# The low parts of the Mamba layer's weights: subtracted by VectorE, or added by a transfer onto the negative high part

## The chip, the core and the metric

The kernel runs on one core of a Trainium2 chip. Five engines take part: TensorE multiplies matrices (in the profile PE for the products and PEld for the loads of the stationary operand), VectorE (DVE), ScalarE (ACT) and GpSimd (POOL) do the elementwise work, and SyncE (SP) begins most transfers; transfers themselves are moved by 16 DMA engines. Every engine works through its own instructions in the order in which the program gives them. The metric is the device time of one launch in microseconds (us); less is better.

## The reference, cut to what matters

A two-layer streaming encoder runs on 512 prompt frames and 32 sample frames, taken together as 544 columns. The first layer is a feed-forward half step, a Mamba-2 mixer, another feed-forward half step and a gated input embedding; the second layer has attention in the mixer's place. The change touches only the Mamba-2 mixer:

```python
def mamba2_mixer(h, ssm0, conv0, w_in, conv_w, conv_b, dt_bias, a_log, d_skip, norm_g, w_out):
    zxbcdt = h @ w_in
    z = zxbcdt[..., :D_INNER]
    ...
    xbc, conv_new = causal_dwconv(xbc, conv0, conv_w, conv_b)
    xbc = jax.nn.silu(xbc).astype(jnp.float32)
    ...
    y, s_fin = ssd_scan(xs * dt[..., None], dt * A, Bm, Cm, s0, chunk_len)
    y = y + xs * d_skip...
    y = y.reshape(b, L, D_INNER) * jax.nn.silu(z.astype(jnp.float32))
    ...
    out = y.astype(h.dtype) @ w_out
```

All of it is float32. The two products with `w_in` (1024 by 5152) and `w_out` (2048 by 1024) are what the change concerns: how their weights get into the form in which TensorE takes them.

## The kernel before

**High and low parts.** A float32 product is made from three products in the reduced type float32r: each weight tile `raw` (128 partitions by 1024 columns, 512 KB) is split into a high part `whi`, which is `raw` rounded to float32r, and a low part `wlo`, which is `raw` minus `whi`, rounded again. The activations are split likewise. `product` (line 282) then makes, for each 128 by 128 block, the products high by high, high by low and low by high, each in two halves of 272 columns: 48 matrix instructions for a tile.

**The Mamba stage.** `mamba` (line 938) lists its weight tiles in `units`, 58 of them: one for the time steps, 24 for the convolved inputs (for each of four groups B, C and four x tiles), 16 for the gates z, 16 for the output, and one that belongs to the feed-forward block that follows. `dense` (line 1115) goes through them in order and gives TensorE a tile's products as soon as the tile is split. The first tile comes split from the stage before, so 57 are split here. Beside the products runs the scan, `ssd` (line 1326), for four groups of five chunks each: transposes and small products on TensorE; on ScalarE the decays `ex` and `ab` by exponentials; on VectorE the evictions and multiplications by decays; on GpSimd the products `xw`, `ab` and `st`. For each chunk SyncE fetches `ab` (line 1163), a table of running sums, repeated to all partitions. The scan's results go through a gated norm (`gnorm`, line 1343) and become the activations of the output tiles.

**Feed.** The class `Feed` (line 311) has two chains. `fetch` (line 318) begins the transfer of tile after tile from SyncE into one of two `raw` buffers. `split` (line 330) waits for the tile, takes one of two `w` slots (a pair of buffers `whi` and `wlo`), copies `raw` into `whi` on ScalarE or GpSimd, subtracts on VectorE or GpSimd, and gives the `raw` buffer back. `dense` gives the `w` slot back when the tile's products are given out.

**What sets the order.** The order of each engine's instructions is made by a planner, the class `Plan` (line 65), while the program is built. Every piece of work is a chain, a generator that asks for slots, for events, or for time on an engine: `T`, `V`, `S`, `G` stand for TensorE, VectorE, ScalarE and GpSimd, `W` for VectorE without the port that it shares with GpSimd in the planner's account. `run` (line 137) always takes the step that can start first by the planner's own clock, among equals the chain of lowest rank, and writes down its instruction then. `copy` (line 306) and `either` (line 302) choose the engine that the planner holds to be less loaded, with GpSimd's time weighted by 7 in this stage. A transfer of a tile is booked as landing after 4.5 us, one of `ab` after 5.0 us. On the chip each engine keeps that order and waits where the planner's clock was wrong. The chain of `split` has rank -2, that of `fetch` -3, the scan's from 1 on, `dense` 50.

Of the kernel before, what the change touches and what calls it, by code (L numbers as in the profile page):

```python
# [5 lines left out]
F32R = mybir.dt.float32r  # L6
BF16 = mybir.dt.bfloat16
AF = mybir.ActivationFunctionType
ALU = mybir.AluOpType

P = 128
D = 1024
# [9 lines left out]
W = 547  # L22
# [22 lines left out]
NZB, NY, NYH = 1, 2, 4  # L45
# [19 lines left out]
class Plan:  # L65
# [9 lines left out]

    LAG = {"TT": 0.0, "TS": 0.2, "TV": 0.2, "TG": 0.23, "ST": 0.28, "SS": 0.143, "SV": 0.142, "SG": 0.17,
           "VT": 0.26, "VS": 0.128, "VV": 0.127, "VG": 0.155, "GT": 0.28, "GS": 0.075, "GV": 0.068, "GG": 0.096}
    LOAD = 1.3  # L80

    def __init__(self, slots, name):
        self.share = SHARE[name]
        self.busy = dict.fromkeys("TVSG", 0.0)
        self.port = 0.0
        self.slots = {k: [0.0] * n for k, n in slots.items()}
        self.events, self.chains, self.table = {}, [], None
# [27 lines left out]
    def start(self, c):  # L115
        kind, t = c["req"][0], c["t"]
        if kind == "get":
            free = self.slots[c["req"][1]]
            return max(t, min(free)) if free else None
        if kind == "wait":  # L120
            when = [self.events.get(e) for e in c["req"][1:]]
            return None if None in when else max([t] + when)
        kind, port = ("V", 0.0) if kind == "W" else (kind, self.port if kind in "VG" else 0.0)
        t = max(t + (self.LAG[c["on"] + kind] if c["on"] else 0.2), self.busy[kind], port)
        table = c["req"][3] if len(c["req"]) > 3 else None
        return t + (self.LOAD if table not in (None, self.table) else 0.0)

    def load(self, engine):

        kinds = "VW" if engine in "VW" else engine  # L130
        return self.busy["V" if engine == "W" else engine] + sum(c["req"][1] for c in self.chains if c["req"][0] in kinds)

    def pick(self, *options):
# [3 lines left out]
    def run(self):  # L137
        while self.chains:
            best = None
            for c in self.chains:  # L140
                t = self.start(c)
                if t is not None and (best is None or t < best[0] - 1e-9):
                    best = t, c
            assert best is not None, "no chain can go on"
            t, c = best
            kind = c["req"][0]
            if kind == "get":
                free = self.slots[c["req"][1]]
                free.remove(min(free))
                c["t"] = t  # L150
            elif kind == "wait":
                if t > c["t"]:
                    c["on"] = None
                c["t"] = t
            else:
                c["req"][2]()
                if len(c["req"]) > 3:
                    self.table = c["req"][3]
                if kind in "VG":
                    self.port = t + c["req"][1]  # L160
                kind = "V" if kind == "W" else kind
                c["t"] = self.busy[kind] = t + c["req"][1]
                c["on"] = kind
            self.step(c)
# [6 lines left out]
def s_cost(n, psum=False):  # L171
    return n / 1200.0 + (0.052 if psum else 0.094)


def v_cost(n):
    return n / 960.0 + 0.069


def _body(tc, io):
# [3 lines left out]
    class Engine:  # L183


        def __init__(self, name, engine):
            self.name, self.engine = name, engine
# [9 lines left out]
    V, S, G, TE = (Engine(n, e) for n, e in (("V", nc.vector), ("S", nc.scalar), ("G", nc.gpsimd), ("T", nc.tensor)))  # L197
# [4 lines left out]
    with ExitStack() as ctx:  # L202
# [66 lines left out]
        def weight_parts(pool=pool):  # L269
            return [pool.tile([P, 1024], F32R, tag=t, name=t, bufs=2) for t in ("whi", "wlo")]  # L270
# [27 lines left out]
        def split(dst_hi, dst_lo, src):  # L298
            S.activation(dst_hi, src, AF.Copy)
            V.tensor_tensor(out=dst_lo, in0=src, in1=dst_hi.bitcast(F32), op=ALU.subtract)  # L300

        def either(plan, cost_v, cost_g, emit):

            return plan.pick(("V", cost_v, lambda: emit(V)), ("G", cost_g, lambda: emit(G)))

        def copy(plan, n, out, src):

            return plan.pick(("S", s_cost(n), lambda: S.activation(out, src, AF.Copy)),
                             ("G", (0.055 + n / 960.0) * (1.0 if n <= 544 else 0.9), lambda: G.tensor_scalar(out, src, 1.0, 0.0, op0=ALU.mult, op1=ALU.add)))

        class Feed:


            def __init__(self, plan, aps, ready=(), here=0):
                self.plan, self.aps, self.ready, self.here = plan, aps, len(ready), len(ready) + here
                self.raw, self.loaded = {}, dict(enumerate(ready))

            def fetch(self):
# [11 lines left out]
            def split(self):  # L330
                for k in range(len(self.aps)):
                    if k < self.ready:
                        yield "get", "w"
                        yield "set", (self, k)
                        continue
                    yield "wait", (id(self), "raw", k)
                    yield "get", "w"
                    raw = self.raw[k]
                    hi = pool.tile([P, 1024], F32R, tag="whi", name="whi", bufs=2)
                    yield copy(self.plan, 1024, hi, raw)  # L340
                    lo = pool.tile([P, 1024], F32R, tag="wlo", name="wlo", bufs=2)
                    yield either(self.plan, v_cost(1024), 2.4, lambda e: e.tensor_tensor(out=lo, in0=raw, in1=hi.bitcast(F32), op=ALU.subtract))
                    self.loaded[k] = hi, lo
                    yield "put", "raw"
                    yield "set", (self, k)


        class Norm:
# [33 lines left out]
            def scale(self, psum, ring):  # L382
                if self.share is not None:
                    self.r = self.share.r
                else:
                    parts = ring() if ring else [self.acc]
                    if ring:
                        split(*parts, self.acc)
                    self.r = at_once(rsqrt_ops(psum(), parts, D, "r", sign=-1 if ring else 1))
                return self.r  # L390
# [505 lines left out]
        def sevens(i, norm, after, bank, tmp, ring, roles, **kw):  # L896
            slots = {f"b{k}": 1 for k in range(4)}
            slots.update({f"c{k}": 1 for k in range(4)})
            slots.update({"raw": 2, "w": Sevens.NW, "a11": 1, "a21": 1, "a22": 1, "a12": 1, "s3": 1, "s2": 1, "gu0": 1, "gu1": 1, "sq": 2, "acc": 1, "h": NH})
            return Sevens(Plan(slots, "ff"), i, norm, bank, tmp, ring, roles, after, **kw).run()  # L900
# [37 lines left out]
        def mamba(norm, after, ready, ahead):  # L938
            with tc.tile_pool(name="mt", bufs=1, reuse_waits="tile") as tmp, \
# [6 lines left out]
                def aux():  # L946
                    return pa.tile([P, 512], F32, tag="aux", name="aux")

                plan = Plan({"mm": 2, "aux": 4, "raw": 2, "w": 2, "cu": 2, "cv": 2, "grp": 2, "z": NZB, "y": NY, "yh": NYH,
                             "ab": 2, "ex": 2, "xd": 2, "xw": 2, "cb": 1, "btok": 1, "st": 3, "fade": 2}, "m")  # L950
                chunks = [(c * P, P) for c in range(NCH)] + [(TP, TS)]
                tok = tmp.tile([P, 5, 96], F32, tag="tok", name="tok")
# [147 lines left out]
                units = [(io["win"][40], "dt", 0, 0)]  # L1100
# [299 lines left out]
                        yield "wait", ("z", g, 0), *[("out", g, c) for c in range(5)]  # L1400
                        yield from gnorm(g)

                feed = Feed(plan, [u[0] for u in units], ready, 1)
                for g in range(NG):
                    plan.add(RSCAN * g + 1, ssd(g))
                    for c in range(5):
# [515 lines left out]
        def space(name, side=None):  # L1922
            st = ExitStack()
            return st, st.enter_context(tc.tile_pool(name=name, bufs=1, reuse_waits="tile", **({"side": side} if side else {})))

        def ring_of(pool, tag, n):
            return lambda: tuple(pool.tile([P, T], F32R, tag=tag + k, name=tag + k, bufs=n) for k in "hl")

        sp, psum, bank, roles = banks(START[0])
        st, tmp = space("ff")  # L1930
# [9 lines left out]
        ready = sevens(0, n00, nm0.ops, bank, tmp, ring_of(tmp, "h", NH), (2, 3, 1, 0), opened=opened, ahead=io["win"][40])  # L1940
        st.close()
        sp.close()
        n01 = Norm("f01")
        ready = mamba(nm0, n01.ops, ready, io["wgu"][1, 0, 0])

        kvp = ctx.enter_context(tc.tile_pool(name="kvp", bufs=1, reuse_waits="tile"))
# [18 lines left out]
        st, tmp = space("pl")  # L1965
# [12 lines left out]
        st, tmp = space("ff")  # L1978
        ready = sevens(2, n10, nm1.ops, bank, tmp, ring_of(tmp, "h", NH), roles(), first=first, ahead=io["wq"][0])
# [3 lines left out]
        ready = attention(nm1, n11.chunk, ready, io["wgu"][3, 0, 0], *kvs)  # L1983
# [3 lines left out]
        st, tmp = space("pl")  # L1987
# [124 lines left out]
```

## Time and profile before

| what | value |
|---|---|
| median of three runs | 2340.38 us (2337.31 to 2341.64) |
| the profiled execution's own time | 2335.02 us |
| its span, first to last instruction | 2332.9 us |
| busy in the span: PE, PEld | 2295.5 us, 2206.8 us |
| busy in the span: DVE, ACT, POOL | 1707.0 us, 1045.5 us, 599.3 us |
| read from HBM | 204.83 MB |
| transfers begun by GpSimd | none |

The times of the profile are those of one execution, in microseconds from its first instruction. An engine's busy time is the time in which it ran at least one of its instructions. Since matrix instructions overlap, PE shows as busy where it only drains; the loader PEld stands still as soon as the next product can't start, so its idle time tells more of TensorE's pauses. "Idle before" names the instruction whose end let the waiting one go.

### The profile page before, as it was taken

To read this page: it belongs to the slowest core of one execution; us is meant where nothing else is said; L and a number is where in the kernel's file an instruction comes from. 1 tells how busy PE (TensorE), PEld (TensorE's weight loads), DVE (VectorE), ACT (ScalarE), POOL (GpSimd) and SP (SyncE) were. 2 spreads that over 40 slices of the span, in tenths; PEclk is the share of its full clock that TensorE was granted. 3 is DMA by queue.
4 is the path that set the end of the run, shared out by engine and by line. 5 is a ranking of instruction groups with operands and counts; after the bars stand their busy time and mean duration, and the time that the engine had idled before them with its cause. 6 is when DMAs were issued, how large, how long until landed. Compare 5 with 4: busy or idle time off the path is not lost.

```text
span 2332.9 us, 42534 instructions
## 1 busy us (share of the span) xinstructions
PE 2295.5 (98%) x17750; PEld 2206.8 (95%) x17757; DVE 1707.0 (73%) x2237; ACT 1045.5 (45%) x1528; POOL 599.3 (26%) x570
## 2 busy tenths in 40 slices
PE   8999999999999999999999999999998999999997
PEld 8999999989899999999999999999964799999997
DVE  7677786689677676777857677777678686777857
ACT  5333334567555453333345433333478553333343
POOL 3322122144324122212211221211334122222214
PEclk9999999999999999999999999999999999999998
DMA  4233323333333232333233333232311132333232
GB/s 159 83 99 105 96 66 90 112 98 99 112 91 90 82 118 84 90 108 91 73 101 100 110 100 95 89 107 67 88 41 32 37 118 78 105 96 99 65 104 75
DMA packets 112176, 213.17 MB, mean 91 GB/s; under 512 B 12528, under 2 KB 34672, under 8 KB 111984
## 3 DMA queue, kind: packets, MB, share of 16 engines
q1 hardware_dynamic: 109104, 204.92, 29.5%
q10 hardware_dynamic: 2880, 5.53, 0.7%
q8 instruction: 140, 2.29, 0.4%
q14 instruction: 52, 0.43, 0.1%
HBM read 204.83 MB, written 5.60 MB: 90 GB/s over the span
## 4 chain that ended last, share of the span: by engine, by line
PE 89%; DVE 5%; ACT 2%; issue 2%; POOL 1%; DMA 1%; SPq 0%; DVEq 0%; ACTq 0%; POOLq 0%
PE mm L191 80%; PE z L191 5%; PE aux L191 2%; PE f L191 1%; DVE wlo L191 1%; PE o L191 1%; POOL ab L191 1%; DVE xl L191 1%; ACT whi L191 1%; DVE x L191 1%; DMA x<-in_x 0%; DVE sl L191 0%; DMA wraw<-in_wpg 0%; DVE fu L191 0%; POOL st L191 0%
## 5 line engine op out<-in xcount | busy, mean ns | idle before, releaser
L191 PE MATMUL mm<-xh,whi 128*128 128x272 f32 x2096 | 512.2, 292 | 0.8 <-ACT xh L191 0.4
L191 PE MATMUL mm<-xl,whi 128*128 128x272 f32 x2096 | 508.0, 290 | 4.4 <-DVE xl L191 4.4
L191 PE MATMUL mm<-xh,wlo 128*128 128x272 f32 x2096 | 505.9, 289 | 2.1 <-DVE wlo L191 2.1
L191 PEld LDWEIGHTS mm<-xh,whi 128*128 128x128 f32 x2096 | 358.1, 189 | 8.9 <-issue 7.0
L191 ACT ACTIVATE whi<-wraw 128x1024 fp32r<-128x1024 f32 (+3 forms) x219 | 188.0, 859 | 392.6 <-PE mm L191 271.7
L191 PEld LDWEIGHTS mm<-xl,whi 128*128 128x128 f32 x2096 | 358.2, 190 | 5.5 <-DVE xl L191 5.5
L191 PEld LDWEIGHTS mm<-xh,wlo 128*128 128x128 f32 x2096 | 358.0, 189 | 2.9 <-DVE wlo L191 2.9
L191 PE MATMUL mm<-xfh,whi 128*128 128x272 f32 x1152 | 332.0, 288 | 0.0
L191 PE MATMUL mm<-xfl,whi 128*128 128x272 f32 x1152 | 331.9, 288 | 0.0
L191 PE MATMUL mm<-xfh,wlo 128*128 128x272 f32 x1152 | 331.7, 288 | 0.0
L191 DVE TENSOR_TENSOR wlo<-wraw,whi 128x1024 fp32r<-128x1024 f32 (+3 forms) x253 | 258.5, 1022 | 71.0 <-ACT whi L191 53.4
L191 PE MATMUL mm<-hh,whi 128*128 128x272 f32 x1408 | 291.2, 288 | 0.0
L191 PE MATMUL mm<-hh,wlo 128*128 128x272 f32 x1408 | 291.0, 288 | 0.0
L191 PE MATMUL mm<-hl,whi 128*128 128x272 f32 x1408 | 290.7, 288 | 0.0
L191 ACT ACTIVATE whi<-a 128x1024 fp32r<-128x1024 f32 x126 | 133.8, 1062 | 310.9 <-PE mm L191 202.8
L191 DVE TENSOR_TENSOR wlo<-a,whi 128x1024 fp32r<-128x1024 f32 x144 | 176.5, 1226 | 102.1 <-ACT whi L191 68.8
L191 PEld LDWEIGHTS mm<-hl,whi 128*128 128x128 f32 x1408 | 221.2, 188 | 0.0
L191 PEld LDWEIGHTS mm<-hh,whi 128*128 128x128 f32 x1408 | 220.9, 188 | 0.0
L191 PEld LDWEIGHTS mm<-hh,wlo 128*128 128x128 f32 x1408 | 220.5, 188 | 0.2 <-DVE wlo L191 0.2
L191 PEld LDWEIGHTS mm<-xfh,wlo 128*128 128x128 f32 x1152 | 216.8, 188 | 0.0
L191 PEld LDWEIGHTS mm<-xfl,whi 128*128 128x128 f32 x1152 | 216.8, 188 | 0.0
L191 PEld LDWEIGHTS mm<-xfh,whi 128*128 128x128 f32 x1152 | 216.7, 188 | 0.0
(293 smaller groups left out, 4200.5 us busy)
## 6 DMA issues: line engine op xcount, KB each, us to landing
a<-in_wgu SPq DMA_DIRECT2D x144, 512.0 KB, 3.9
wraw<-in_wd SPq DMA_DIRECT2D x128, 256.0 KB, 2.7
wraw<-in_win SPq DMA_DIRECT2D x41, 512.0 KB, 3.6
wraw<-in_wgu SPq DMA_DIRECT2D x30, 512.0 KB, 3.6
wraw<-in_wd SPq DMA_DIRECT2D x32, 384.0 KB, 3.1
ab<-acs_d SPq DMA_DIRECT2D x16, 512.0 KB, 4.3
wraw<-in_wout SPq DMA_DIRECT2D x16, 512.0 KB, 3.6
wraw<-in_wpg SPq DMA_DIRECT2D x16, 512.0 KB, 3.6
```

The lines of the kernel that those rows point to most:

```text
L191: ins = getattr(self.engine, op)(*args, **kw)
```

## The change

In the Mamba stage alone, `Feed` gets a pool `third` and takes another way. ScalarE writes the negative high part into the low part's buffer (`lo`, an activation with scale -1 whose output type rounds). GpSimd then begins a transfer that reads the same weight tile from HBM a second time and adds it to that buffer. The high part is copied as before, on ScalarE or GpSimd. VectorE's subtraction (or GpSimd's) is gone. The planner books 0.9 us on GpSimd for beginning the transfer (the new kind `D`, which counts on GpSimd without the shared port) and counts the tile as ready 5.5 us later, by a chain of its own. The `raw` buffer goes back once both copies are made. There are three `w` slots instead of two, the third pair of buffers from the stage's own pool; the last three tiles use only the two old pairs, since these outlive the stage.

```diff
+    ON = {"W": "V", "D": "G"}
...
-        kind, port = ("V", 0.0) if kind == "W" else (kind, self.port if kind in "VG" else 0.0)
+        kind, port = (self.ON[kind], 0.0) if kind in "WD" else (kind, self.port if kind in "VG" else 0.0)
...
-        kinds = "VW" if engine in "VW" else engine
+        kinds = {"V": "VW", "W": "VW", "G": "GD", "D": "GD"}.get(engine, engine)
...
-                kind = "V" if kind == "W" else kind
+                kind = self.ON.get(kind, kind)
...
-            def __init__(self, plan, aps, ready=(), here=0):
-                self.plan, self.aps, self.ready, self.here = plan, aps, len(ready), len(ready) + here
+            def __init__(self, plan, aps, ready=(), here=0, third=None):
+                self.plan, self.aps, self.ready, self.here, self.third = plan, aps, len(ready), len(ready) + here, third
...
                     raw = self.raw[k]
+                    if self.third is not None:
+
+                        third = k % 3 == 2
+                        if third and k >= len(self.aps) - 3:
+                            yield "get", "w"
+                            third = False
+                        hi, lo = self.loaded[k] = (tuple(self.third.tile([P, 1024], F32R, tag=t, name=t) for t in ("whi", "wlo")) if third else weight_parts())
+
+                        yield "S", s_cost(1024), lambda: S.activation(lo, raw, AF.Copy, scale=-1.0)
+                        yield "D", 0.9, lambda: G.dma_start(lo, self.aps[k], accum_op=ALU.add)
+                        yield "spawn", self.landed(k)
+                        yield copy(self.plan, 1024, hi, raw)
+                        yield "put", "raw"
+                        yield "set", (self, "hi", k)
+                        continue
...
+            def landed(self, k):
+                yield "sleep", 5.5
+                yield "wait", (self, "hi", k)
+                yield "set", (self, k)
...
-                plan = Plan({"mm": 2, "aux": 4, "raw": 2, "w": 2, "cu": 2, "cv": 2, "grp": 2, "z": NZB, "y": NY, "yh": NYH,
+                plan = Plan({"mm": 2, "aux": 4, "raw": 2, "w": 3, "cu": 2, "cv": 2, "grp": 2, "z": NZB, "y": NY, "yh": NYH,
...
-                feed = Feed(plan, [u[0] for u in units], ready, 1)
+                feed = Feed(plan, [u[0] for u in units], ready, 1, third=tmp)
```

## The prediction

> **What bounds the kernel now.** I read the page first: PE is busy for 98% of the span, and PE makes up 89% of the chain that ended last.
>
> ```profile
> span 2332.9 us, 42534 instructions
> PE 2295.5 (98%) x17750; PEld 2206.8 (95%) x17757; DVE 1707.0 (73%) x2237; ACT 1045.5 (45%) x1528; POOL 599.3 (26%) x570
> PE 89%; DVE 5%; ACT 2%; issue 2%; POOL 1%; DMA 1%; SPq 0%; DVEq 0%; ACTq 0%; POOLq 0%
> ```
>
> So the change can only win time in which TensorE pauses. The timeline gives the limits of the Mamba stage: its first product begins at 385.67 us, and the first one of the block behind it at 827.15, hence 441 us.
>
> ```profile
> 385.67 0.42 PE L191 MATMUL mm<-xh,whi 128*128 128x272 f32 x2
> 827.15 0.42 PE L191 MATMUL mm<-xh,whi 128*128 128x272 f32 x2
> ```
>
> Next I cut these 441 us into windows by hand, at the points where the scan of a group sets in or ends. Columns: window, its length, then busy time (and instructions) of each engine, granted clock, DMA share, GB/s.
>
> ```profile
> 386.00:440.00 54.00, 54.00 (x427) 53.51 (x425) 42.65 (x81) 26.10 (x33) 12.69 (x28) 1.00 0.30 92
> 440.00:500.00 60.00, 58.24 (x483) 52.59 (x484) 41.29 (x82) 41.42 (x73) 24.59 (x26) 0.98 0.41 121
> 500.00:545.00 45.00, 45.00 (x348) 44.36 (x347) 36.57 (x63) 25.31 (x37) 10.78 (x30) 0.98 0.27 79
> 545.00:640.00 95.00, 92.56 (x791) 82.23 (x789) 75.73 (x144) 65.71 (x126) 44.42 (x36) 1.00 0.39 110
> 640.00:700.00 60.00, 60.00 (x465) 59.10 (x465) 43.21 (x67) 29.62 (x41) 13.31 (x26) 0.97 0.32 92
> 700.00:760.00 60.00, 59.61 (x482) 54.43 (x482) 42.07 (x80) 32.92 (x61) 25.64 (x15) 0.94 0.31 87
> 760.00:827.00 67.00, 67.00 (x531) 66.84 (x531) 45.01 (x54) 28.44 (x38) 13.77 (x9) 1.00 0.29 85
> sum 441.00, PE 436.40 PEld 413.06 DVE 326.52 ACT 249.52 POOL 145.20; mean PE 62.34 PEld 59.01 DVE 46.65 ACT 35.65 POOL 20.74
> ```
>
> The loader column tells the most. In 386 to 440, 500 to 545, 640 to 700 and 760 to 827 it is within 1 us of the window's length: nothing can be won there. The pauses lie in the three windows of the scans, and all of the loader's idle time is 441.0 - 413.1 = 27.9 us. Who ends it is in the views of who waited for whom in these 441 us, the loader's first, then TensorE's own:
>
> ```profile
> PEld mm L191 <- issue: 9.0, 31, 0.8
> PEld aux L191 <- issue: 6.0, 23, 0.9
> PEld aux L191 <- POOL xw L191: 2.7, 6, 1.1
> PEld aux L191 <- POOL ab L191: 1.6, 3, 1.0
> PEld aux L191 <- DVE wlo L191: 0.8, 1, 0.8
> PE aux L191 <- POOL xw L191: 1.4, 2, 0.9
> PE aux L191 <- POOL ab L191: 1.2, 2, 0.9
> PE aux L191 <- DVE btok L191: 0.8, 1, 0.8
> ```
>
> 15.0 us have no releaser ("issue": the loader is free, but the product ahead of it is a long one), and no other engine can give them back. To an engine's name go the loader's 5.1 us shown here and 1.1 us in rows under 0.8, and 4.5 us of TensorE's own idle time (441.0 - 436.4). The ceiling of this change is therefore about 6.2 + 4.5 = 10.7 us, 0.46% of the kernel. That is the frame for everything below.
>
> **The change part by part.** Removed: the subtractions.
>
> ```profile
> L191 DVE TENSOR_TENSOR wlo<-wraw,whi 128x1024 fp32r<-128x1024 f32 x57 | 74.1, 1300 | 12.5 <-ACT whi L191 9.1 <-POOL whi L191 2.9
> L191 ACT ACTIVATE whi<-wraw 128x1024 fp32r<-128x1024 f32 x48 | 50.8, 1059 | 88.9 <-PE mm L191 67.4 <-issue 16.3 <-POOL yh L191 4.4
> ```
>
> 57 times 1.300 is 74.1 us, so VectorE falls from 326.5 to 252.4 us of 441. All of it lies beside products; on the path is only what a scan step waits behind it. The rows name VectorE with 0.8 (`wlo`), 0.8 (`btok`) and some 1.5 us in small rows: I count 3.1 us as won. The larger part is indirect. GpSimd, which ends 2.7 + 1.6 + 1.4 + 1.2 = 6.9 us of TensorE's waits, itself waits for VectorE:
>
> ```profile
> POOL ab L191 <- DVE fade L191: 34.8, 10, 7.3
> POOL xw L191 <- DVE xd L191: 34.5, 8, 12.2
> ```
>
> With 23% of VectorE's work gone (74.1 of 326.5), `xd` and `fade` come earlier. How much arrives is not in the trace: between nothing and all 6.9 us; I take half, 3.5. Gross gain 6.6 us.
>
> There is a second way by which GpSimd gains. Its operations are stretched at times:
>
> ```profile
> L191 POOL TENSOR_TENSOR xw<-xd,tok x20: 1032/1055/2031, 443.7 to 742.3; 128x512 f32<-128x512 f32 x16, 32x512 f32<-32x512 f32 x4
> ```
>
> Shortest and median agree at 1.05 us, the longest takes 2.03: something holds it. [...] I leave the half as it is.
>
> Added on ScalarE, for which the largest scan window counts, here the subtractions in it alone (busy time of VectorE and their number), and a wait of VectorE for ScalarE:
>
> ```profile
> 545.00:640.00 95.00, 13.21 (x9) 1.00 0.39 110
> DVE ex L191 <- ACT ex L191: 16.7, 13, 3.6
> ```
>
> There are 57 negative copies. Their nearest row is the positive copy above, 1.059 us each, so 60.4 us, and ScalarE goes from 249.5 to 309.9 us of 441 (70%). In the quiet windows that is hidden beside products. In the scans it is less so: 545 to 640 has ScalarE at 65.7 of 95, and nine tiles more (the subtractions there) make 75.2, just where VectorE stood with 75.7. Each chunk needs three pieces of ScalarE (`ex`, its exponential, `ab`), 60 in all; a copy is in front with a chance of 60.4/441 = 14% and half of 1.06 us left, so 60 x 0.14 x 0.53 = 4.5 us of delay, of which I let a third reach TensorE: 1.5 us lost. (From below nothing, from above all 4.5.)
>
> Added on GpSimd: 57 beginnings of transfers. The trace has none begun by GpSimd. The nearest rows bound one: SyncE's issue of a tile (0.33) below, GpSimd's longest kind of product (`ab`, 2.39) above; I take 1.0 us, near `xw`.
>
> ```profile
> L266 SPq DMA_DIRECT2D wraw<-in_win x38: 327/328/600, 390.2 to 746.9; - x38
> L191 POOL TENSOR_TENSOR ab<-ab,C x16: 740/2394/2979, 467.2 to 745.1; 128x1024 f32<-128x1024 f32 x12, 128x256 f32<-128x256 f32 x4
> L191 POOL TENSOR_TENSOR st<-st,fade x16: 1032/1212/2031, 469.6 to 748.0; 128x512 f32<-128x512 f32 x16
> ```
>
> That is 57 us (19 to 136), and GpSimd goes from 145.2 to about 202 of 441. Queued behind a beginning, which also waits for ScalarE's copy, are `xw`, `ab` and `st` (20 + 16 + 16 = 52), for which the scan's products wait: 52 x 0.13 x 0.5 = 3.4 us, a third of it on TensorE: 1.1 us lost (0.1 to 6.4 by the bounds; the upper one is a third of 52 x 0.31 x 1.2).
>
> Added on the DMA engines: 57 times 512 KB, 29.9 MB beside the stage's present traffic, and two reads for each write.
>
> ```profile
> L1163 SPq DMA_DIRECT2D ab<-acs_d x20: 359/377/575, 439.2 to 728.5; - x20
> DMA packets 31066, 42.67 MB, mean 97 GB/s; under 512 B 5553, under 2 KB 22193, under 8 KB 31025
> wraw<-in_win SPq DMA_DIRECT2D x38, 512.0 KB, 3.6
> ab<-acs_d SPq DMA_DIRECT2D x16, 512.0 KB, 4.3
> a<-in_wgu SPq DMA_DIRECT2D x4, 512.0 KB, 6.5
> ```
>
> By bytes the traffic grows by 0.70; the share of 0.27 to 0.41 in the windows becomes about 0.5 to 0.7 if an added byte costs like a plain one, and 0.65 to nearly 1 if it costs two: room, but little. An accumulating landing isn't in the trace. Below stands the plain tile, 3.6 us; above, twice the slowest group here, 13. I take 5.5, a plain tile and half of one again.
>
> What covers it is the third slot. In the row below, 390 products take 48.98 us, 0.1256 each, so a tile of 48 keeps TensorE for 6.03 us.
>
> ```profile
> 390.51 48.98 PE mm L191 x390
> ```
>
> A freed slot is needed again two tiles later, in 12 us (6 with two slots). From that go the copy (1.1), the beginning (1.0) and about 1 us of queueing on both engines: 9 us are left for the landing. With 5.5 nothing shows; without the third slot each tile would be 2.6 us late. The high copy and the return of `raw` run beside it. `fetch` and SyncE keep their work; the wait on a freed buffer moves from VectorE's to ScalarE's end. Nothing changes outside the stage.
>
> Sum: -3.1 - 3.5 + 1.5 + 1.1 = **-4.0 us**. The profiled execution took 2335.02 us, of which 2332.9 are span; the median of the runs is 2340.38. Four microseconds less than that median is **2336.4 us**. The forecast's own range is 2330 to 2342 (10.7 won at best; with GpSimd's term at its upper bound, 6.6 won and 1.5 + 6.4 lost).
>
> **The rivals.** *ScalarE takes VectorE's place.* For it: 75.2 us of 95 in the largest scan, and the 16.7 us in which VectorE already waits for ScalarE's `ex` (row above); against it: ScalarE stood blocked for 67.4 us behind slots that products had not yet freed (row of the copies), and that wait is shorter with three slots. Then the gain goes, and the result is 2340 (2337 to 2343).
>
> *Transfers collide and `ab` comes late (slower).* The scan's `ab` lands in 4.3 us in the middle; the planner counts on 5.0 and puts ScalarE's work in that order. The accumulating transfers take the same DMA engines. If they add 2.0 us to each of 20 landings, 1.3 us each lie beyond the 5.0: 26 us on ScalarE in the scans, half of it on TensorE: +13, 2353 us. It decides from a landing of 5.0 us on for `ab`, or of 9 us for a low part, beyond which every tile pays. For it speak the 6.5 us that the crowded group above took; against it, that no window now has a DMA share over 0.41.
>
> *VectorE holds back GpSimd's beginnings (slower).* If each has to wait for VectorE's running instruction, 57 x 0.57 (its remaining share of 441) x 0.5 us are 16 us on GpSimd, a third of it on TensorE: +5, and with the other terms 2341 to 2348. [...]
>
> *The ceiling is reached.* The planner orders everything anew, and the scans close all named pauses, 10.7 us, and some of the 15 us: 2327.
>
> **How the numbers follow.** A measurement of this kernel can tell about 0.2%, 4.7 us, from no change. Forecast 0.50: 0.28 of it beyond 4.7 us, 0.22 within. ScalarE instead 0.20: 0.16 within, 0.02 on each side. Collision 0.18: 0.17 slower, 0.01 within. Held back 0.04, slower. Ceiling 0.08, faster. Together faster 0.38, same 0.39, slower 0.23. The range is 2325 to 2353: below it little is possible, and above lies about a tenth, the worse half of the collisions.
>
> **What would show it.** Right: VectorE at about 252 us between the first product and the next block, ScalarE near 310, GpSimd near 200, PEld's idle time in the three scan windows some 4 us less, low parts landing within 9 us, no wait of TensorE named after a transfer into `wlo`. Wrong: such waits; `ab` landing beyond 5 us and ScalarE's `ex` waiting for it; GpSimd's beginnings over 2.4 us; waits on ScalarE's copies where VectorE's stood. The forecast falls if quiet windows show loader gaps: then the landing, not the scan, has become the bound.

## The result: slower by 0.28%

| kernel | median us | lowest to highest | runs | ratio to before, 95% interval |
|---|---|---|---|---|
| before | 2339.51 | 2337.31 to 2341.64 | 8 | |
| after | 2346.95 | 2342.12 to 2348.86 | 8 | 1.0028 [1.0018, 1.0039] |

The change makes the kernel about 7.4 us slower; the forecast was 4.0 us faster. One execution of a kernel below, e3, took 3701.07 us at a granted clock of 0.555; it is left out of that kernel's ratio and means. The head of the page of after:

```profile
span 2340.4 us, 42581 instructions
PE 2300.2 (98%) x17757; PEld 2210.7 (94%) x17757; DVE 1646.1 (70%) x2182; ACT 1109.3 (47%) x1597; POOL 612.8 (26%) x615
PE 89%; DVE 4%; ACT 3%; issue 2%; DMA 2%; POOL 1%; SPq 0%; DVEq 0%; ACTq 0%; POOLq 0%
```

VectorE has lost 60.9 us and ScalarE gained 63.8, as the change intends, and "DMA" in the chain went from 1 to 2%. The profiled execution took 2342.12 us, the fastest of its eight, so a profile of after shows less than the median's loss. Its windows of the Mamba stage (length, busy time of PE, PEld, DVE, ACT, POOL, granted clock, DMA share, GB/s):

```profile
386.00:440.00 54.00, 50.61 (x375) 49.70 (x375) 30.86 (x72) 35.37 (x42) 13.55 (x37) 0.94 0.78 185
440.00:500.00 60.00, 58.14 (x493) 53.09 (x491) 30.00 (x67) 47.73 (x79) 25.19 (x31) 1.00 0.68 166
500.00:545.00 45.00, 45.00 (x361) 43.81 (x360) 37.59 (x70) 37.34 (x54) 16.23 (x37) 1.00 0.70 159
545.00:640.00 95.00, 92.87 (x785) 83.25 (x785) 62.84 (x130) 77.50 (x134) 43.90 (x44) 1.00 0.69 162
...
sum 445.00, PE 436.44 PEld 413.06 DVE 264.81 ACT 314.41 POOL 154.91; mean PE 62.35 PEld 59.01 DVE 37.83 ACT 44.92 POOL 22.13
```

Look at the first row. Before, TensorE was busy for all of its 54.00 us at full clock; now 3.4 us are idle and the clock is 0.94. This was a quiet window, in which by the forecast nothing could change. The scan at 545 to 640 is hardly better (PE 92.87 against 92.56). The waits of the stage, the loader's and TensorE's (waiting tile, what it waited for, us in all, times, longest):

```profile
PEld mm L193 <- issue: 9.7, 32, 0.8
PEld aux L193 <- POOL xw L193: 4.7, 7, 1.6
PEld aux L193 <- issue: 4.2, 19, 0.8
PEld mm L193 <- DMA wlo<-in_win: 3.6, 1, 3.6
PE mm L193 <- DMA wlo<-in_win: 3.4, 1, 3.4
PE aux L193 <- POOL xw L193: 3.2, 5, 1.4
```

VectorE's `wlo` and `btok` and GpSimd's `ab` (1.6 and 1.2 us before) are gone from the list, but GpSimd's `xw` went up (2.7 to 4.7, 1.4 to 3.2), and one single stop of 3.4 us (3.6 as the loader sees it) stands behind a low part's transfer. The timeline shows where (start, length, engine, operation; in brackets the idle time before and what ended it):

```profile
388.62 1.05 ACT L193 ACTIVATE wlo<-wraw 128x1024 fp32r<-128x1024 f32 x1
389.98 1.04 POOL L193 DMA_DIRECT2D wlo<-in_win  x1 [3.79 <-ACT wlo L193]
393.65 0.41 PE L193 MATMUL mm<-xl,whi 128*128 128x272 f32 x2
395.78 1.06 ACT L193 ACTIVATE wlo<-wraw 128x1024 fp32r<-128x1024 f32 x1 [3.27 <-DMA wraw<-in_win]
397.45 0.82 PE L193 MATMUL mm<-xh,wlo 128*128 128x272 f32 x2 [3.39 <-DMA wlo<-in_win]
```

The stage's first product is at 386.45 (385.67 before). Only the first weight tile comes split from the stage before; the second has its negative copy at 388.62, its beginning at 389.98, and its low part is there at 397.45. TensorE had come to it at 394.06 (393.65 + 0.41). So 5.4 us were at hand for copy, beginning and landing, and 8.8 were needed. Behind the stop the products run at little more than half speed: a pair of them comes every 0.45 us, against 0.25 ahead of the stop. Two windows there:

```profile
394.00:397.40 3.40, 0.06 (x1) 0.00 (x0) 0.00 (x0) 1.62 (x2) 0.27 (x1) 0.89 1.05 231
397.40:403.00 5.60, 5.55 (x24) 5.55 (x25) 3.22 (x7) 2.53 (x4) 0.58 (x1) 0.50 1.05 256
```

Last, the queues of the stage (packets, MB, share of 16 engines' time), the landings, and the beginnings on GpSimd:

```profile
q0 software_dynamic: 8208, 29.89, 41.4%
q1 hardware_dynamic: 28985, 38.71, 25.6%
...
wlo<-in_win POOLq DMA_DIRECT2D x40, 512.0 KB, 5.8
wraw<-in_win SPq DMA_DIRECT2D x38, 512.0 KB, 5.7
ab<-acs_d SPq DMA_DIRECT2D x16, 512.0 KB, 6.1
```

```profile
L193 POOL DMA_DIRECT2D wlo<-in_win x40 | 35.5, 888 | 140.4 <-ACT wlo L193 132.8 <-DVE fade L193 6.0 <-ACT ex L193 1.5
```

q0 holds the low parts alone. A plain tile lands in 5.7 us in the middle (3.6 before), `ab` in 6.1 (4.3).

### The profile page after: what moved, and what is told of

Same layout as the page of the kernel before. It is cut to its first block, busy times and chain, and to the rows that moved or that the text cites. A ratio compares the mean times of both kernels' runs of the same rounds, so it can differ in the third digit from the quotient of the medians.

```text
span 2340.4 us, 42581 instructions
## 1 busy us (share of the span) xinstructions
PE 2300.2 (98%) x17757; PEld 2210.7 (94%) x17757; DVE 1646.1 (70%) x2182; ACT 1109.3 (47%) x1597; POOL 612.8 (26%) x615
## 3 DMA queue, kind: packets, MB, share of 16 engines
q0 software_dynamic: 8208, 29.89, 7.9%
## 4 chain that ended last, share of the span: by engine, by line
PE 89%; DVE 4%; ACT 3%; issue 2%; DMA 2%; POOL 1%; SPq 0%; DVEq 0%; ACTq 0%; POOLq 0%
PE mm L193 79%; PE z L193 5%; PE aux L193 2%; PE f L193 1%; PE o L193 1%; DVE wlo L193 1%; ACT whi L193 1%; DVE xl L193 1%; DVE x L193 1%; DMA ab<-acs_d 0%; ACT ex L193 0%; DVE fu L193 0%; DMA wraw<-in_wpg 0%; DMA wlo<-in_win 0%; DVE sl L193 0%
## 5 line engine op out<-in xcount | busy, mean ns | idle before, releaser
L193 ACT ACTIVATE whi<-wraw 128x1024 fp32r<-128x1024 f32 (+3 forms) x228 | 196.8, 864 | 309.6 <-PE mm L193 204.4
L193 DVE TENSOR_TENSOR wlo<-wraw,whi 128x512 fp32r<-128x512 f32 (+3 forms) x196 | 185.8, 948 | 58.4 <-ACT whi L193 44.1
```

Source lines behind the costliest of these rows:

```text
L193: ins = getattr(self.engine, op)(*args, **kw)
```

## The experiments

Theory: the loss is made at the stage's entry, by the late first low part and by the third slot that is open from the start, and in the scans VectorE's relief brings nothing. Rivals: the transfers collide with `ab` and slow the scans; or the scans do gain, and something larger hides it.

All runs in one table. Each ratio is against runs of before made alongside (their medians are 2338.7 to 2339.0), since 2339.51 belongs to after alone. "Stage" is, in the profiled execution, from the first product of the Mamba stage to the first of the block behind it; "half clock" is the time in it at a granted clock of 0.50, from the record of the clock (half of it is counted as lost; in after a pair of products comes every 0.45 us there, against 0.25 at 1.00, so this is an estimate, a little high). These two are of one execution. The last two columns are of all: the record has the mean granted clock of each execution, and one minus it, times the span, is what the clock took at most. "Clock" is the mean of this loss, "rest" the mean time without it, both in us more than before's alongside. Their standard errors are about 1.5 and 0.8 us.

| run | low parts | third slot | median us | ratio, 95% interval | stage | half clock | clock | rest |
|---|---|---|---|---|---|---|---|---|
| before | VectorE | none | 2339.51 | | 441.5 | 13.7 |  |  |
| e2 | VectorE | none | 2337.81 | 0.9998 [0.9989, 1.0006] | 439.8 | 13.7 | -0.3 | +0.1 |
| after | transfer | from the start | 2346.95 | 1.0028 [1.0018, 1.0039] | 444.8 | 13.7 |  |  |
| e7 (= after) | transfer | from the start | 2345.03 | 1.0027 [1.0018, 1.0036] | 444.0 | 10.2 | +3.4 | +3.1 |
| e4 | transfer | none | 2375.62 | 1.0164 [1.0148, 1.0179] | 479.1 | 37.5 | +10.6 | +26.9 |
| e1 | three tiles VectorE, then transfer | from the start | 2340.82 | 1.0007 [0.9997, 1.0018] | 442.0 | 13.7 | +0.3 | +1.0 |
| e3 | VectorE | from the start | 2342.54 | 1.0018 [1.0009, 1.0027] | 445.2 | 27.3 | +7.0 | -3.0 |
| e10 | transfer | after the norm | 2342.03 | 1.0019 [1.0010, 1.0027] | 443.4 | 6.8 | +2.2 | +2.3 |
| e8 | three tiles VectorE, then transfer | after the norm | 2337.50 | 0.9992 [0.9984, 1.0001] | 441.6 | 17.1 | -0.2 | -1.2 |
| e9 | VectorE | after the norm | 2334.63 | 0.9987 [0.9979, 0.9996] | 438.9 | 13.7 | -1.0 | -1.7 |
| e5 | plain transfer | from the start | 2342.20 | 1.0021 [1.0012, 1.0030] | 447.0 | 23.9 | +3.9 | +0.9 |
| e12 | copies alone | after the norm | 2340.21 | 1.0005 [0.9996, 1.0014] | 444.5 | 20.5 | +3.1 | -1.3 |
| e11 | none from the fifth tile | after the norm | 2345.48 | 1.0024 [1.0015, 1.0033] | 449.7 | 34.1 | +6.5 | -0.8 |
| e13 | none, but booked | after the norm | 2334.57 | 0.9987 [0.9978, 0.9996] | 438.8 | 17.1 | +2.1 | -4.9 |

**e1, e2, e3: which part of the change loses.** e2 is before once more, a measure of what two equal kernels differ by. e1 gives the first three tiles that the stage splits (k up to 3) back to VectorE:

```diff
+                        if k <= 3:
+                            yield copy(self.plan, 1024, hi, raw)
+                            yield either(self.plan, v_cost(1024), 2.4, lambda e: e.tensor_tensor(out=lo, in0=raw, in1=hi.bitcast(F32), op=ALU.subtract))
+                            yield "put", "raw"
+                            yield "set", (self, k)
+                            continue
```

> Theory 1 (the entry): nearly all of the 7.4 us that the changed kernel loses come from the stage's entry, where the first low part lands at 397.4 us though TensorE needs it at 394, a stop of 3.4 us, and from the half clock that follows it for 6.8 us, another 3.4 us; the scans neither win nor lose. Here the first three split tiles get their low parts from VectorE as in the kernel before, the other 54 by the accumulating transfer. Theory 1 expects no stop of TensorE for a transfer into wlo near 395 us, no half clock there, and the time of the kernel before within 2 us (2338 to 2342). Theory 2 (busy DMA engines: tiles and ab land 2 us later all through the stage) and theory 3 (ScalarE's 60 us more delay the scans) put the loss in the scans and expect it to stay: 2344 to 2347.

> The kernel before, once more, for the scatter. All theories expect a ratio of 1.000 within 0.1%. The profile tells whether stretches at half clock outside the Mamba stage, which the changed kernel's profile has at the start and in attention (two of 6.8 us there) and the profile of before has not, come and go from run to run: if they do, this profile may have some too.

e1 takes back 5 of the 7 us (1.0028 to 1.0007), and the stop behind the low part is gone. The other 54 tiles go by transfer, with `ab` landing in 5.9 us, as late as in after, so a collision in the scans is not what loses the most. In its place e1 has a stop of 2.4 us of a kind that before hasn't: a product waits for `dv`, made by VectorE behind the norm's `r`. e3 shows that this comes from the third slot. It has three slots, open from the start, and all low parts from VectorE (`if True:` for `if k <= 3:`).

> All 57 low parts by VectorE as before, but with three pairs of buffers in turn: the third slot alone. Theory 1 expects the time of before within 2 us, since nothing stops TensorE for weights in the kernel before; if the third slot by itself helps the scans, it would show as up to 3 us less, and if the split running a tile further ahead crowds VectorE in the scans, as more.

e3 is 0.18% slower than before without any transfer begun by GpSimd, against the 2 us that theory 1 allowed. It has such a stop too, of 1.6 us. Its timeline at the entry:

```profile
393.20 0.49 ACT L193 ACTIVATE ry<-aux,epsb 128x272 f32<-128x272 f32 x1
...
395.58 1.06 ACT L193 ACTIVATE whi<-wraw 128x1024 fp32r<-128x1024 f32 x1 [1.89 <-DMA wraw<-in_win]
396.54 0.47 ACT L193 ACTIVATE ry<-aux,epsb 128x272 f32<-128x272 f32 x1
...
399.80 0.72 DVE L193 SCALAR_TENSOR_TENSOR r<-rm,ry 128x544 f32<-128x544 f32 x1
```

With a free slot the planner puts the copy of the third tile that is split here between the two halves of the norm's `ry`, since it books a transfer as landed after 4.5 us. The tile isn't there, ScalarE stands for 1.89 us, and with it the norm behind. `r` comes at 399.80; without that copy in between it is e9's, below:

```profile
393.06 0.87 ACT L193 ACTIVATE ry<-aux,epsb 128x272 f32<-128x272 f32 x2
...
396.30 1.06 ACT L193 ACTIVATE whi<-wraw 128x1024 fp32r<-128x1024 f32 x1 [2.38 <-DMA wraw<-in_win]
396.97 0.72 DVE L193 SCALAR_TENSOR_TENSOR r<-rm,ry 128x544 f32<-128x544 f32 x1
```

In after the same tile's copies stand ahead of the norm (395.78, with 3.27 us of waiting, above); TensorE's own stop covers their effect. The stop of 2.4 us fits e1's rest (1.0 us, against -1.2 of e8 below, which lacks it), but a stop doesn't explain e3's time: e3's rest is 3.0 us less than before's, and all of its loss is in the clock, with stretches at half clock that begin at 489, 578, 643 and 756 us, none at the entry. Why there are more of them isn't shown.

**e4: how much the third slot covers.** The change with two slots (`"w": 2`, and `third = False`).

> The changed kernel with two pairs of buffers instead of three. By the prediction's budget (6.0 us for a tile, from which go 1.1 for the copy, 1.0 for the beginning, 1 of queueing and now 5.7 of landing) each tile is 2.8 us late in the quiet stretches, some 30 tiles: 85 us, and with half clocks behind the stops more: 2430 us or above. If the landing were not on the path with two slots either, the time would stay near 2347.

```profile
PEld mm L193 <- DMA wlo<-in_win: 15.0, 13, 3.9
PE mm L193 <- DMA wlo<-in_win: 12.1, 10, 3.7
```

38 us slower than before (1.64%), or 0.7 us for each of 57 tiles; 90 and more were expected. TensorE's stops behind low parts are 12.1 us here and 2.3 for the output's weights; 23.8 us more at half clock cost another 12. The other 12 us or so are not located.

**e8, e9, e10: the entry mended in steps.** The third slot opens only when the norm's `r` is made:

```diff
-                plan = Plan({"mm": 2, "aux": 4, "raw": 2, "w": 3, ...
+                plan = Plan({"mm": 2, "aux": 4, "raw": 2, "w": 2, ...
...
+                def third_slot():
+                    yield "wait", "r"
+                    yield "put", "w"
+                plan.add(49, third_slot())
```

e10 is after with this alone; e8 has e1's first tiles as well; e9 makes all low parts on VectorE.

> With the entry's first three tiles by VectorE the loss fell from 7.4 to about 2 us, and that kernel's profile still has a stop of 2.4 us near 398 us: the third slot lets ScalarE take up a third tile whose transfer has not landed, in front of the second half of the norm's reciprocal root, so that the eviction of the first product comes late. Here the third slot also opens only when that norm is done. Theory 1 (all the loss lies at the entry) expects that stop gone too and 2336 to 2340, the time of before or up to 2 us less; theories 2 and 3 (a small loss in the scans from late transfers or ScalarE's load) expect 2340 to 2343 as without the late slot.

> All low parts by VectorE, three slots, the third one opened after the norm. Against the kernel with the entry mended this leaves only the way of the low parts as a difference: 54 subtractions of VectorE against 54 copies, beginnings and transfers. If VectorE's relief is worth something in the scans, as the prediction had it (3 to 7 us), this one is slower than that by as much; theory 1 expects the two within 2 us of each other, both at 2336 to 2340.

> The changed kernel with the late third slot alone: the first low parts still come by transfer. Theory 1 expects the stop for the first tile to stay (3.4 us or, with one raw tile fewer under way, some 2 us less) and the half clock behind it (3.4 us); the second tile, which now gets its slot as before, may be late as well. 2343 to 2350. If the third slot's crowding were the main cause instead of the landing, the time would be 2340 or less.

The four kernels make a ladder. From before to e9 (third slot, late, no transfers): -0.13%, 3.0 us; of the kernels that leave no work out it is the only one whose interval lies below before. From e9 to e8 (transfers from the fourth split tile on): +0.05%, within the intervals. From e8 to e10 (the first three by transfer too): +0.27%, about 6 us. From e10 to after (third slot open from the start): +0.09%, 2 us, within the intervals. So most of the loss comes with the first low parts. (e9 came out under the 2336 to 2340 expected, and e10 under its 2343 to 2350, without a half clock at the entry.) One caution: the planner orders each kernel anew, and the order alone can be worth more than these steps (e11 and e13, below). In the traces TensorE's products stand in nearly the same order in e8 and e10 (97% of them in one sequence), but not in e9 and e8 (64%), so the step from e8 to e10 is a fair price, and the 0.05% holds for transfers and another order together. e10's timeline has the same stop as after:

```profile
389.67 1.04 ACT L193 ACTIVATE wlo<-wraw 128x1024 fp32r<-128x1024 f32 x1
391.04 1.04 POOL L193 DMA_DIRECT2D wlo<-in_win  x1 [3.81 <-ACT wlo L193]
...
398.51 0.52 PE L193 MATMUL mm<-xh,wlo 128*128 128x272 f32 x2 [3.40 <-DMA wlo<-in_win]
```

The products behind it run at full clock here (1.00 from 398 to 402; 0.52 us for this pair against 0.82 in after).

**e5, e12: what the accumulation and the transfers cost.** e5 leaves out `accum_op=ALU.add`: a plain transfer begun by GpSimd, so that the low part holds the whole weight. e12 is e8 without the transfers (`"D"` and `landed` left out): the low part holds the negative high part.

> The changed kernel with a plain transfer in the place of the accumulating one: it writes the weight tile over the negative high part, so the low part holds the whole weight and the outputs are not the reference's; all copies, beginnings and bytes from HBM stay. If the accumulation makes the landing long (5.7 us against 3.6 of a plain tile), it falls to 3.5 to 4.5 here, the queue's share of the DMA engines from 41% of the stage to about half, and the stop at the entry to under 2 us: 2339 to 2344. If a transfer begun by GpSimd is slow in itself, landing and time stay at 5.7 and 2347.

> The mended entry and the late slot, the negative copies on ScalarE from the fifth tile on, but no transfers: the low part is left as the negative high part, so the outputs are not the reference's. Against the kernel with the same entry and the transfers (2337.5) it shows what the transfers cost by their landing, their beginnings and the busy DMA engines; against the kernel without any work for low parts what ScalarE's 57 us cost. Theory 1 expects all three within 4 us; theory 2 expects this one 3 us or more under 2337.5; theory 3 expects it 3 us or more above the one without low parts.

e5's queues and landings (columns as for after):

```profile
q1 hardware_dynamic: 29008, 38.80, 27.2%
q0 software_dynamic: 8076, 29.41, 24.3%
...
wlo<-in_win POOLq DMA_DIRECT2D x40, 512.0 KB, 4.0
wraw<-in_win SPq DMA_DIRECT2D x39, 512.0 KB, 4.7
ab<-acs_d SPq DMA_DIRECT2D x16, 512.0 KB, 4.8
```

A plain transfer lands in 4.0 us instead of 5.8, and `ab` in 4.8 instead of 6.1. Yet e5's 1.0021 lies within the intervals of after and e10: its stop behind the low part is only 0.4 us, but now one for `dv` shows, which in after, as I read it, the stop for the low part had covered:

```profile
PE mm L193 <- DVE dv L193: 4.6, 1, 4.6
...
PE mm L193 <- DMA wlo<-in_win: 0.4, 1, 0.4
```

And e12, without any of the transfers, is not faster than e8 but 0.13% slower (the intervals overlap). Its rest is e8's (-1.3 and -1.2); what differs is the clock. That the 29.9 MB cost time in the scans has thereby no support; since the planner orders e12's work anew, e12 doesn't prove that they cost nothing.

**e11, e13: what VectorE's relief is worth.** From the fifth tile on e11 has no low-part work at all (`lo = hi`; TensorE multiplies by the high part twice). e13 does the same, but keeps the subtraction in the plan without giving out its instruction, so that all other work stands in e9's order (TensorE's products agree to 99% in the traces, with e11's to 80%). In both the third slot opens late and the first tiles go as in e9:

```diff
+                        if k > 3:
+                            lo = hi
+                            self.loaded[k] = hi, lo
+                            yield copy(self.plan, 1024, hi, raw)
+                            yield either(self.plan, v_cost(1024), 2.4, lambda e: None)
+                            yield "put", "raw"
+                            yield "set", (self, k)
+                            continue
...
```

> From the fifth tile on no low part is made at all: the third product of each block takes the high part again, so TensorE's work is the same, and neither VectorE nor ScalarE nor GpSimd nor the DMA engines do anything for low parts (the outputs are not the reference's). The third slot opens after the norm. This is the most that any way of taking low parts off VectorE could bring. The prediction's working would have it 7 to 11 us under the kernel with VectorE's subtractions and the late slot (2334.6): 2324 to 2328. Theory 1 (the scans are bound by TensorE; VectorE's relief is worth next to nothing) expects 2331 to 2336.

> As e9 (all low parts booked on VectorE, third slot opened by the norm), but from the fifth tile of weights on the subtraction is booked by the planner and not issued: VectorE has no low-part work there, TensorE multiplies by the high part in the place of the low part, so the output is not the reference's, and the order of all other work is that of e9. e11, where the low parts were not booked either, took 2345.5 against e9's 2334.6, with 17.1 us of half-clock loss in its Mamba stage against 6.8. Theory 'order': e11 lost through the planner's other order; with e9's order kept the relief of VectorE shows by itself, and the time is at or below e9's: 2328 to 2336 us, stage 433 to 440 us; what it lies below 2334.6 is all that freeing VectorE of the low parts can be worth. Rival 'relief': a freed VectorE lets TensorE's waits fall so that the clock is halved more often, in any order: 2342 to 2348 us, with 12 us or more of half-clock loss in the stage. Between (2336 to 2342): neither is shown.

The sums over 386 to 831, first of e9, then of e13, then some windows of e11: two slices about the start of a half-clock stretch, and the largest scan:

```profile
sum 445.00, PE 442.04 PEld 418.33 DVE 326.37 ACT 259.79 POOL 149.50; mean PE 442.04 PEld 418.33 DVE 326.37 ACT 259.79 POOL 149.50
```

```profile
sum 445.00, PE 442.71 PEld 420.34 DVE 267.13 ACT 257.51 POOL 118.47; mean PE 442.71 PEld 420.34 DVE 267.13 ACT 257.51 POOL 118.47
```

```profile
480.80:484.10 3.30, 3.30 (x28) 2.35 (x26) 3.30 (x7) 0.00 (x0) 2.44 (x4) 1.00 0.56 166
484.10:490.90 6.80, 6.80 (x32) 6.55 (x33) 5.11 (x14) 5.12 (x7) 2.04 (x4) 0.50 0.61 170
...
545.00:640.00 95.00, 90.22 (x728) 79.05 (x727) 56.08 (x121) 65.70 (x117) 35.34 (x31) 0.93 0.36 103
```

VectorE goes from 326.4 to 267.1 us, and the time stays: both ratios are 0.9987, with intervals of 0.09% (2 us) each way. GpSimd goes from 149.5 to 118.5 us though none of its work is left out: its `xw` of 128x512 takes 1045 ns for 1267, its `cstate` 289 for 585. So beside the subtractions GpSimd's instructions had run longer: the gain that the prediction has as its second way is there. Counted without the loss at half clock, e13's stage is 1.8 us shorter than e9's in the profiles (438.8 - 8.5 against 438.9 - 6.8); over all executions its rest is 3.2 us less (-4.9 against -1.7, give or take 1.0), and its loss to the clock 3.1 us more (give or take 1.9). By this count 59 us off VectorE bring TensorE some 3 us, and the clock takes about as much. e11 was a miss: with the same work left out it is 10.9 us slower than e13. Only the order differs. Of the 10.9 us between the two profiled stages, 8.5 are the 17 us more at half clock; over all executions the clock has 4.5 of 8.6 us. Why its order halves the clock more often stays open: in its largest scan TensorE is busy for 90.22 of 95 us, where e9 had 92.59 and e13 92.99, but the stretch at 484.10 begins behind a slice in which it shows no idle time (3.30 of 3.30). An order of e11's work with more even scans wasn't tried.

**e7: after once more**, beside e11 and e12.

> The changed kernel once more, for a second profile on this chip. Theory 1 expects a ratio near 1.003, the stop of 3.4 us for the first low part in the same place, and a stretch at half clock behind it in this profile too, or, where it is missing, a stage shorter by 3 us.

Its 1.0027 repeats the result; its stop behind the first low part is 3.9 us, with 3.4 us of half clock behind it.

## Why the prediction was wrong

**The failed step: the cover of the landing.** "9 us are left for the landing", and with 5.5 "nothing shows". The size was near: 5.7 us in the middle, 5.3 to 9.3. But the 12 us of a slot's turn hold only once the chain is running ahead. The stage enters with one split tile, and then 5.4 us are at hand, from which 1.4 pass until GpSimd starts the beginning. Even the 5.5 assumed would have been 1.4 us late; the first landing took 7.5 us (389.98 to 397.45), with the DMA share at 1.05 in the last part of it, where plain tiles land beside it. Before, the subtraction took 1.2 us there. e8 against e10 prices this step at 0.27%, some 6 us: 3.4 us (give or take 1.1) in the rest, which is the length of the first stop, and 2.4 (give or take 2) in the clock. "The forecast falls if quiet windows show loader gaps" is what happened, in the first window, which had been read as one where nothing can be won; it could be lost there.

**The gain: -3.1 and -3.5.** No time came of either. The wait for `wlo` did vanish, and `xw` waited less for `xd` (14.3 us against 34.5; `ab` for `fade` as before, 35.7 against 34.8), but TensorE's waits for `xw` rose. e13 is the clean measure: VectorE relieved by 59 us with the order kept, some 3 us less in the rest, which the clock took back. The 6.6 were also counted too high to begin with, for the loader's and TensorE's waits are in part the same stops. Two lines of before:

```profile
489.83 0.29 PEld L191 LDWEIGHTS aux<-xw,btok 32*128 32x128 f32 x2 [1.14 <-POOL xw L191]
489.83 1.12 PE L191 MATMUL aux<-xw,btok 32*128 32x512 f32 x2 [0.90 <-POOL xw L191]
```

Both wait for one `xw`. Counted once, GpSimd's 6.9 us are 4.3, and the ceiling of 10.7 is some 8 us. The share of a wait was taken as time won when its releaser gets faster; it would have needed the question what comes last next, and some 14 us of "issue" stand in before (15.0) as in after (13.9).

**The third slot as mere cover.** e4 shows that it is needed, though 0.7 us a tile and not 2.6. What was missed is that a free slot also lets the planner begin a tile early, ahead of the norm, on a transfer that isn't there. Open from the start it costs 0.31% with VectorE's low parts (e3 against e9), but all of that is in the clock (8 us more lost over all executions, 6.8 in the profiles), and its stretches at half clock lie in the scans: that the early copy is their cause isn't shown. With transfers it is some 2 us (after against e10), within the intervals. Opened late, the slot wins 0.13%, together with the order that comes of it.

**ScalarE +1.5, GpSimd +1.1.** ScalarE at 314.4 us (309.9 expected) and beginnings of 0.89 us (1.0) were sized well; VectorE at 264.8 lies above the 252.4. GpSimd's 154.9 lie far below 202: its nine high copies are gone (10.6 us), its beginnings took 50 us, and stretches in which two of its instructions overlap count once (the times of its groups add up to 182). What these terms cost is within e8 against e9, 0.05% for both, the other order and all else in the scans.

**The rivals.** The collision came true in its condition (`ab` at 6.1 us, past the 5.0), not in its price: ScalarE's `ex` waited for `ab` 2.6 us in all, where 26 were feared, and e8, with `ab` at 5.6, is no slower than before. Its second point, 9 us for a low part, was set too high for the entry, where 7.5 were too late. ScalarE in VectorE's place fits the scans of e8, not the loss. GpSimd's beginnings waited for VectorE once for 6.0 us (row of the beginnings), not 57 times.

**What stays open.** The two profiles of after have a stage 3.8 us longer than the two of before (444.4 against 440.6 on average), nearly the stop itself, and their executions differ by 4.2 us, while the medians differ by 6 to 7. The remaining 2 to 3 us are in executions that no profile shows, and their clock tells of them: e7's executions take 6.4 us more than before's in the mean, 3.1 (give or take 0.8) in the rest and 3.4 (give or take 1.4) by the clock. So about half of the loss stands in the rest, near the stop in size, and about half is more time at a reduced clock. Where in those executions it lies, and why, stays open, as does why a change of order changes it.

## What to carry to other kernels

Cover that a ring of buffers gives holds in its steady turn; before a longer latency goes into a chain, work out the first two or three turns at each stage's entry, where the ring is empty, and keep the short way for them. Here an engine that is 74% busy and named in some waits was relieved of a fifth of its work, and no time was won: a trial that books the work but leaves it out, with the order kept, gives the worth of a relief ahead of the work to move it. Before waits are added up, look whether two rows are the same stop. A new free slot is also a new licence for the planner: bind its opening to the work that must go first. And where the clock of every execution is on record, part each time into what the clock took and the rest, before a difference of a few microseconds is explained.

## What the runs showed of the hardware

**An accumulating transfer's price.** In after the low parts take 41.4% of the DMA engines' time for 29.89 MB, the plain traffic of queue q1 25.6% for 38.71 MB: 2.1 times as much for a byte. Begun by GpSimd without accumulation (e5), 29.41 MB take 24.3%, so 1.7 times is the accumulation's own. Its neighbours are slower too: plain tiles land in 5.7 us in after, in 4.7 in e5, and in 3.6 in before, which has no transfer begun by GpSimd.

**The clock.** Behind stops of 3.39 and 3.92 us TensorE's granted clock was 0.50, for 6.8 us in after and 3.4 in e7; behind one of 3.40 us it stayed at 1.00 (e10). The clock's record goes in steps of 3.41 us: in the step before the fall TensorE stood for 2.6 us of it in after and for 2.2 in e7, while e10's stop is spread over two steps, with 1.8 and 1.6 us. So the length of a stop alone doesn't settle it. The three agree with a fall where more of one step is idle, but three stops don't prove it, and neither of the two steps before a fall was idle throughout. Stretches of 3.4 to 10.2 us at half clock come in the stage of every version (6.8 us in all in e10, 37.5 in e4). Idle time doesn't explain them all: before the one that begins at 498 us in before, TensorE shows as busy for all of the 3.41 us. What does explain them isn't shown. In the profiles they are worth up to 8.5 us between two orders of the same work (e11, e13).
